# Four modulation pieces of state-space groups 0 to 2 computed beside the value products, in buffers reserved for the softmax rows

## The chip, the cores and the metric

The kernel runs on one core of a Trainium2 chip. The metric is device time in microseconds (us) of one launch. Five engines work beside each other, each through its own queue of instructions in order: TensorE (PE; its weight loads are counted apart as PEld), VectorE (DVE), ScalarE (ACT), GpSimd (POOL) and SyncE (SP), which here issues most DMAs. An instruction that waits holds back all that stands behind it on its engine.

## The reference, cut to what matters

One layer over 512 latent tokens and 256 context tokens, width 1024:

```
mod = silu(c) @ w_mod + b_mod                 # 6 x 1024 modulation values
sh1, sc1, gt1, sh2, sc2, gt2 = split(mod, 6)
h_lat, h_ctx = modulate(x, norm1_g, sh1, sc1), modulate(ctx, ...)
p = h @ w_in                                  # z | x,B,C | dt | q | k | v | gates
ssd  = ssd_bidir(...)                         # 4 groups of 8 heads, chunks of 128 tokens
att  = window_ctx_attention(q, k, v, ...)     # 16 heads, 4 for k and v
x = x + gt1 * ((g_ssd*(ssd @ w_o_ssd) + g_att*(att @ w_o_att)) @ w_out)
x = x + gt2 * conv_ffn(modulate(x, norm2_g, sh2, sc2))
return rmsnorm(x, final_g)
```

The first two of the six parts of `mod` (sh1, sc1) are needed at the start; the other four (gt1 on) only after both branches are merged. `w_mod` for these four is 16 MB.

## The kernel before

**Products.** Matrices are in fp32. Every product is made from two rounded halves of each operand: high × high, high × low, low × high (L197, L198, L200). A 512 KB piece of weights is loaded by SP into a ring of three buffers (`wraw`, L145); ScalarE casts it to the high half `whi` (L149), VectorE subtracts to get the low half `wlo` (L150). In attention the same pair of operations stands at L941 and L944. `hlh`, `hll`, `hch`, `hcl` are the halves of the normalised latent and context tokens, already transposed.

**Stages.** Start and modulation of the first part to 54 us; first products for q and k to 77 us; value products 77 to 95.8 us; attention to about 330 us with other products between; the output of attention; the four state-space groups g0 to g3, about 405 to 735 us; merging, output, the feed-forward part. "q2" and "q3" below are the third and fourth weight piece of q, loaded by SP ahead of attention.

**The modulation pieces.** The late four parts of `mod` are 32 pieces of 512 KB, and `m_step(i)` (L571) does one. VectorE multiplies the rows by silu(c) and adds into one tile `tm`: L581 for the first half of the first piece, L583 for each later half, so two operations a piece. After every fourth piece TensorE transposes `tm` in four blocks into a PSUM bank (L591), VectorE reduces that bank to `mod` (L593) and adds the bias (L594). In g0, g1 and g2 three pieces each are done (0 to 8), through the ring `wraw`; the rest follows after the groups.

**Value products** (`v_step`): six row blocks of the tokens, each accumulated in a PSUM bank of its own, five of the pool `mis` and one of the pool `acc` (L693 to L695). Afterwards ScalarE rounds each bank to the high half (L699) and copies 64 further columns (`te`, L701), and VectorE forms the low half (`vst`, L700).

**PSUM.** Eight banks. Up to the value products: three of `acc`, five of `mis`. At the start of attention the pools are laid out anew: two of `acc`, one tile of two banks for the scores, three for transposed probabilities, one for the outputs. The two banks of the scores are the third `acc` bank and the first `mis` bank of the old layout.

**Attention** follows an order written by a planner: scores (L811), softmax rows `p` (L820, L827; seven buffers of 640 columns), transposition to `pth` (L847, L851), product with the values (L860).

**A state-space group** is a list of steps (`prog`). `chunk_in` makes decays: ScalarE adds the time sums (L1465, L1468), VectorE selects (L1469), ScalarE takes the exponential (L1470), VectorE multiplies with the inner products of C and B (L1471), in two halves of four heads. `chunk_out` multiplies with the states (L1480), then with the eight heads' inputs (L1486), and advances the state (L1385, on POOL L1387, and L1388). `chunk_sum` transposes a part onto it (L1504) and multiplies with z (L1506). In between stand the projections of the next group with their convolution (L1267 to L1276) and the modulation pieces. L1365 squares the gated output for the norm. Outside attention the order of the engines' instructions is made by the framework from the order of the program, with a few anchors.

Of the kernel before, what the change touches and what calls it, by code (L numbers as in the profile page):

```python
# [9 lines left out]
F32 = mybir.dt.float32  # L10
F32R = mybir.dt.float32r
U8 = mybir.dt.uint8
AF = mybir.ActivationFunctionType
ALU = mybir.AluOpType
# [4 lines left out]
P = 128  # L19
D = 1024  # L20
L = 512
# [18 lines left out]
def raw(ap):  # L40
    return ap.bitcast(F32)
# [3 lines left out]
def tile_hybrid_layer(  # L45
# [32 lines left out]
    nc = tc.nc  # L78
    V, S, G, T = nc.vector, nc.scalar, nc.gpsimd, nc.tensor
# [17 lines left out]
    def bank(name):  # L97
        pool, w, tag = banks_[name]
        return pool.tile([P, 512 * w], F32, tag=tag, name=tag)
# [8 lines left out]
    def accb():  # L108
        return bank("acc")

    def misb():
        return bank("mis")
# [3 lines left out]
    def tmp(tag):  # L116
        return tpool.tile([P, 512], F32, tag=tag, name=tag, bufs=TMP[tag])
# [21 lines left out]
        src["up", i] = wup[i], 1024  # L139
    src["dn", 0] = wdn[0, 0], 1024  # L140

    def load_raw(key):
        a, n = src[key]
        r = wpool.tile([P, 1024], F32, tag="raw", name="wraw", bufs=3)
        nc.sync.dma_start(r[:, :n], a)  # L145
        return r, n

    def split(r, n, hi, lo):
        S.copy(hi[:, :n], r[:, :n])  # L149
        V.tensor_tensor(lo[:, :n], r[:, :n], raw(hi[:, :n]), ALU.subtract)  # L150

    def split_first(r, n, hi, lo):
        V.tensor_copy(hi[:, :n], r[:, :n])
# [150 lines left out]
    with tc.tile_pool(name="spool", bufs=1) as sp:  # L304
# [131 lines left out]
        r, W, H = {}, {}, {}  # L436
# [50 lines left out]
        rows = {}  # L487
# [47 lines left out]
        for i in range(NG):  # L535
            t = tmp("tb")
# [33 lines left out]
    def m_step(i):  # L570
        cg, kk = i // 4, i % 4  # L571

        def fn(r):
            if kk == 0:
                macc[0] = tmp("tm")
            acc = macc[0]
            for u in range(2):
                k = 2 * kk + u
                sc = csil[:, k, 0:1]
                if k == 0:  # L580
                    V.tensor_scalar_mul(acc, r[:, 0:512], sc)  # L581
                else:
                    V.scalar_tensor_tensor(acc, r[:, u * 512 : u * 512 + 512], sc, acc, ALU.mult, ALU.add)  # L583
            if kk == 3 and cg > 5:
                ps = misb()
                T.matmul(ps, ones, acc, start=True, stop=True)
                V.tensor_tensor(F["g2"][cg - 6], ps, F["g2"][cg - 6], ALU.add)
            elif kk == 3:
                ps = misb()
                for c in range(4):  # L590
                    T.transpose(ps[:, c * P : (c + 1) * P], acc[:, c * P : (c + 1) * P], ident)  # L591
                z = slice(4 * cg, 4 * cg + 4)
                V.tensor_reduce(mod2[:, z], ps.rearrange("p (c q) -> p c q", c=4), axis=AX.X, op=ALU.add)  # L593
                V.tensor_tensor(mod2[:, z], mod2[:, z], vec[:, V_BMOD + 16 + 4 * cg : V_BMOD + 20 + 4 * cg], ALU.add)  # L594

        return [("m", i)], fn
# [5 lines left out]
    a2p = a2pool.enter_context(tc.tile_pool(name="a2pool", bufs=1, reuse_waits="tile"))  # L602
# [59 lines left out]

        return [("k", t)], fn

    Q, F = {}, {}

    def q_high(r, t):
        q = [attp.tile([P, L], F32R, tag="q", name="q", bufs=7) for _ in range(2)]
# [3 lines left out]
    def q_low(r, t):  # L672

        q = Q[2 * t], Q[2 * t + 1]
        lo = tmp("tc").bitcast(F32R)
        V.tensor_tensor(lo, r, raw(q[0]), ALU.subtract)
        for o, i in ((q[1][64:128, :], q[0][64:128, :]), (q[1][0:64, :], lo[64:128, :]), (q[0][64:128, :], lo[0:64, :])):
            nc.sync.dma_start(raw(o), raw(i))

    def q_split(ps, t):  # L680
        r = rope(ps, 1.0)
        q_high(r, t)
        q_low(r, t)

    def v_step(*w):

        pos = [misb() for _ in range(5)] + [accb()]
        for k in range(KT):
            wh, wl = (z[:, (k % 3) * 320 : (k % 3 + 1) * 320] for z in w[k // 3])
            for t, po in enumerate(pos):  # L690
                hh, hl, c0 = (hlh, hll, t) if t < 4 else (hch, hcl, t - 4)
                c, o = slice(c0 * P, (c0 + 1) * P), po[:, 0:320]
                T.matmul(o, hh[:, k, c], wh, start=k == 0, stop=False)  # L693
                T.matmul(o, hh[:, k, c], wl, start=False, stop=False)
                T.matmul(o, hl[:, k, c], wh, start=False, stop=k == KT - 1)  # L695
        steps = tmp("te")
        for t, po in enumerate(pos):
            o = po[:, 0:256].rearrange("p (h d) -> p h d", h=4)
            S.copy(vst[:, t, :, 0:64], o)  # L699
            V.tensor_tensor(vst[:, t, :, 64:128], o, raw(vst[:, t, :, 0:64]), ALU.subtract)  # L700
            S.copy(steps[:, t * 64 : (t + 1) * 64], po[:, 256:320])  # L701
        F["steps"] = steps
# [86 lines left out]
    def block_atoms(n, turned):  # L789
# [27 lines left out]
        def least(i):  # L817
            h = 4 * j + i
            p = d["p"][i] = a2p.tile([P, 640], F32, tag="p", name="p", bufs=NP_)
            V.tensor_tensor_reduce(  # L820
# [57 lines left out]
        def of(k, back):  # L878

            return divmod(k - back, 4) if k >= back else None  # L880

        for i in range(4):
# [5 lines left out]
            needs = ["S%d.%d" % (n, i)] + (["c%d" % (n - 2)] if n > 1 else [])  # L888
            if k >= NP_:
                f, g = of(k, NP_)  # L890
                needs.append("T%d.%d.%d" % (f, (3, 4, 4, 3)[f % 4], g))
# [323 lines left out]

        return some

    NP_ = 7
    BESIDE = [("q", 2), ("q", 3), ("z", 0), ("z", 1), ("k", 1), ("q", 4), ("z", 2), ("z", 3), ("q", 5), ("z", 4)]
    BESIDE += [("q", 6), ("z", 5), ("z", 6), ("q", 7)] + [("z", i) for i in range(7, 14)] + [("oa", 0), ("oa", 1)]  # L1220
    OLD = len(BESIDE)
# [68 lines left out]
    def turn(n=None):  # L1290

        for t, n_, put in TURN[:n]:
            ps = misb()
            for c in range(n_):
                T.transpose(ps[:, c * P : (c + 1) * P], t[:, c * P : (c + 1) * P], ident)
            put(ps)
        del TURN[:n]

    def proj_steps(g):
        d = GR[g]  # L1300

        def b_fn(w):
            d["xs"] = bp.tile([P, 4, 512], F32, tag="xs", name="xs", bufs=2)
            d["xsc"] = bp.tile([P, 2, 512], F32, tag="xsc", name="xsc", bufs=1)
            d["Bkc"] = bp.tile([P, 2, P], F32, tag="Bkc", name="Bkc", bufs=2)
            d["Bk"] = bp.tile([P, 4, P], F32, tag="Bk", name="Bk", bufs=2)
            d["BT"] = bp.tile([P, L], F32, tag="BT", name="BT", bufs=2)
            pl, pc = accb(), accb()
            gemm([LAT(pl)], w)
            turn()  # L1310
            gemm([CTX(pc)], w)
            conv_silu(pl, L, 16 + g, d["BT"])
            BTc = tmp("tc")
            conv_silu(pc, LC, 16 + g, BTc)
            for t, n, k in ((d["BT"], 4, d["Bk"]), (BTc, 2, d["Bkc"])):
                TURN.append((t, n, lambda ps, n=n, k=k: S.copy(flat(k), ps[:, : n * P])))

        def c_fn(w):
            d["CT"] = bp.tile([P, L], F32, tag="CT", name="CT", bufs=2)
            pl = accb()  # L1320
            gemm([LAT(pl)], w)
            turn()
            conv_silu(pl, L, 20 + g, d["CT"])

        def x_fn(ct, w):
            i = 4 * g + ct
            pl, pc = accb(), accb()
            gemm([LAT(pl)], w)
            turn()
            gemm([CTX(pc)], w)  # L1330
            for pp, n, dst in ((pl, L, d["xs"]), (pc, LC, d["xsc"])):
                xl = tmp("tc")
                conv_silu(pp, n, i, xl)
                TURN.append(
                    (
                        xl,
                        n // P,
                        lambda ps, n=n, dst=dst: S.copy(
                            dst[:, :, ct * P : (ct + 1) * P], ps[:, :n].rearrange("p (a b) -> p a b", b=P)
                        ),  # L1340
                    )
                )

        r = [([("x", 16 + g)], b_fn), ([("x", 20 + g)], c_fn)]
        for ct in range(4):
            r.append(([("x", 4 * g + ct)], lambda w, ct=ct: x_fn(ct, w)))
        return r
# [173 lines left out]
        return r + [([], gate)]  # L1521

    msteps = [m_step(i) for i in range(32)]
    prog = proj_steps(0)
    for g in range(4):
        s = ssd_steps(g)
        f = fill[n2 + g : n2 + 1 + g]
        b = proj_steps(g + 1) if g < 3 else fill[n2 + 4 : n3]
        m = msteps[3 * g : 3 * g + 3] if g < 3 else []

        prog += s[0:1] + f + b[0:1] + s[1:2] + m[0:1] + b[1:2]
        for c in range(4):
            prog += s[3 * c + 2 : 3 * c + 3] + (s[3 * c + 4 : 3 * c + 5] if c < 3 else [])
            if g == 3 and c:
                prog += s[3 * c : 3 * c + 1]
            prog += b[2 + c : 3 + c]
            if c == 1:
                prog += b[6:]
            if g < 3 or c == 3:
                prog += s[3 * c + 3 : 3 * c + 4]  # L1540
            if c in (1, 2):
                prog += m[c : c + 1]
        prog += s[13:14]
# [649 lines left out]
```

## Time and profile before

| | us |
|---|---|
| median of 3 runs | 1231.55 |
| lowest, highest | 1231.36, 1231.83 |
| the profiled execution, its whole time | 1231.67 |
| the profiled execution, its span | 1229.8 |
| mean granted clock of TensorE | 0.998 |
| busy: TensorE, its weight loads | 1217.2, 996.6 |
| busy: VectorE, ScalarE, POOL | 914.8, 687.1, 168.0 |

The span runs from the first to the last instruction; the whole time has 1.87 us more around it. "Busy" sums the time of an engine's instructions. In rows of the timeline, the first number is the start and the second the time to the end of the last of so many (x) instructions; the bracket gives the idle time before and what released the instruction. Since instructions are pipelined, a row's end can lie a little behind the next row's start.

### The profile page before, as it was taken

Reading aid. Unit: us, or ns where it says so; the run is one execution under the profiler, and the core shown is the slowest. Engines: PE = TensorE matmul, PEld = TensorE weight load, DVE = VectorE, ACT = ScalarE, POOL = GpSimd, SP = SyncE. Lnnn points to the kernel's source line nnn. Section 1 sums busy time; section 2 is a strip of 40 time slices with the busy share of each in tenths; the row PEclk is TensorE's granted clock in tenths of the full one; section 3 lists DMA queues with packets and bytes.
Section 4 is the critical chain, followed back from the end, with each engine's and each line's share of the span. In section 5 each row is a group of like instructions: output and inputs, shape, how many; then the busy total and the mean of one; then the engine's idle time right before and its main releaser. Section 6 shows DMA issues by size and latency. Waiting matters only on the chain.

```text
span 1229.8 us, 17483 instructions
## 1 busy us (share of the span) xinstructions
PE 1217.2 (99%) x6337; PEld 996.6 (81%) x6337; DVE 914.8 (74%) x1489; ACT 687.1 (56%) x1302; POOL 168.0 (14%) x174
## 2 busy tenths in 40 slices
PE   9999999999999999999999999999999999999997
PEld 6798888888878877777777778888988888888886
DVE  4757888888654698697886786677688788886557
ACT  4657788787443556566586572223544444545543
POOL 0000111121100033233352530000200000000000
PEclk9999999999999999999999999999999999999999
DMA  9653678777846235345346466677144444457785
GB/s 359 250 149 91 216 203 190 213 193 218 219 143 208 92 126 147 117 131 184 122 140 201 137 204 221 230 242 236 50 164 147 145 151 152 153 169 244 245 303 200
DMA packets 108630, 224.65 MB, mean 183 GB/s; under 512 B 9600, under 2 KB 48832, under 8 KB 108544
## 3 DMA queue, kind: packets, MB, share of 16 engines
q1 hardware_dynamic: 101056, 197.32, 49.0%
q0 software_dynamic: 6912, 25.17, 8.7%
q8 instruction: 50, 0.82, 0.3%
q10 hardware_dynamic: 576, 1.05, 0.2%
q14 instruction: 36, 0.29, 0.1%
HBM read 193.29 MB, written 49.87 MB: 198 GB/s over the span
## 4 chain that ended last, share of the span: by engine, by line
PE 92%; DVE 3%; DMA 2%; ACT 2%; issue 1%; SPq 0%; POOLq 0%; ACTq 0%; DVEq 0%
PE acc L197 19%; PE acc L200 19%; PE acc L198 19%; PE acc L1919 3%; PE acc L1917 3%; PE acc L1918 3%; PE score L811 3%; PE po L860 3%; PE pt L847 2%; PE mis L1480 2%; PE mis L1385 2%; DMA wm<-wm 1%; PE acc L930 1%; PE mis L422 1%; PE acc L931 1%; PE acc L932 1%
## 5 line engine op out<-in xcount | busy, mean ns | idle before, releaser
L197 PE MATMUL acc<-hlh,whi 128*128 128x512 f32 x488 | 199.3, 408 | 0.0
L150 DVE TENSOR_TENSOR wlo<-wraw,whi 128x1024 fp32r<-128x1024 f32 (+2 forms) x119 | 143.4, 1207 | 70.1 <-ACT whi L149 60.8
L200 PE MATMUL acc<-hlh,wlo 128*128 128x512 f32 x488 | 191.4, 392 | 0.0
L149 ACT CAST whi<-wraw 128x1024 fp32r<-128x1024 f32 (+2 forms) x119 | 122.6, 1033 | 122.4 <-PE acc L198 74.5
L198 PE MATMUL acc<-hll,whi 128*128 128x512 f32 x488 | 190.8, 391 | 0.0
L197 PE MATMUL acc<-mh,whi 128*128 128x512 f32 x360 | 141.0, 392 | 0.0
L200 PE MATMUL acc<-mh,wlo 128*128 128x512 f32 x360 | 140.1, 389 | 0.0
L198 PE MATMUL acc<-ml,whi 128*128 128x512 f32 x360 | 140.0, 389 | 0.0
L200 PEld LDWEIGHTS acc<-hlh,wlo 128*128 128x128 f32 x488 | 91.6, 188 | 20.4
L198 PEld LDWEIGHTS acc<-hll,whi 128*128 128x128 f32 x488 | 91.9, 188 | 17.5 <-issue 1.7
L197 PEld LDWEIGHTS acc<-hlh,whi 128*128 128x128 f32 x488 | 91.8, 188 | 17.6 <-issue 2.2
L198 PEld LDWEIGHTS acc<-ml,whi 128*128 128x128 f32 x360 | 67.6, 188 | 14.5 <-issue 0.5
L197 PEld LDWEIGHTS acc<-mh,whi 128*128 128x128 f32 x360 | 67.6, 188 | 14.4 <-issue 0.5
L200 PEld LDWEIGHTS acc<-mh,wlo 128*128 128x128 f32 x360 | 67.6, 188 | 14.0
L820 DVE CUSTOM_DVE_ANT_0 p<-score,winm,nsink 128x512 f32<-128x512 f32 (+1 forms) x64 | 51.8, 810 | 15.0 <-PE score L811 13.6
L1268 DVE SCALAR_TENSOR_TENSOR ta<-acc,half,ta 128x511 f32<-128x511 f32 (+1 forms) x66 | 43.8, 663 | 25.8 <-ACT ta L1267 25.8
L1267 ACT ACTIVATE ta<-acc,half 128x512 f32<-128x512 f32 (+1 forms) x66 | 46.8, 709 | 27.1 <-PE acc L200 25.9
L1275 ACT ACTIVATE tb<-ta 128x512 f32<-128x512 f32 (+1 forms) x44 | 23.5, 534 | 65.0 <-DVE ta L1269 59.0
L827 ACT ACTIVATE p<-p,mneg 128x512 f32<-128x512 f32 (+1 forms) x64 | 49.7, 777 | 15.3 <-DVE mneg L820 14.7
L1387 POOL TENSOR_TENSOR st<-st,eT 128x512 f32<-128x512 f32 x24 | 33.5, 1396 | 170.6 <-ACT st L1405 162.3
L197 PE MATMUL acc<-hch,whi 128*128 128x256 f32 x176 | 54.4, 309 | 0.0
L855 DVE TENSOR_TENSOR ptl<-pt,pth 128x512 fp32r<-128x512 f32 x72 | 47.5, 686 | 8.6 <-ACT pth L851 7.8
(512 smaller groups left out, 2972.7 us busy)
## 6 DMA issues: line engine op xcount, KB each, us to landing
wraw<-wup SPq DMA_DIRECT2D x44, 512.0 KB, 3.6
wt_d<-wdn POOLq DMA_DIRECT2D x36, 512.0 KB, 7.5
fb<-cs_d SPq DMA_DIRECT2D x32, 512.0 KB, 6.6
wraw<-wm SPq DMA_DIRECT2D x32, 512.0 KB, 4.3
wraw<-wx SPq DMA_DIRECT2D x24, 512.0 KB, 3.5
wraw<-wt_d SPq DMA_DIRECT2D x20, 512.0 KB, 4.3
sp_d<-te SPq DMA_DIRECT2D x33, 256.0 KB, 2.5
wm<-wm SPq DMA_DIRECT2D x16, 512.0 KB, 7.7
```

The costliest lines, as they stand in the source:

```text
L149: S.copy(hi[:, :n], r[:, :n])
L150: V.tensor_tensor(lo[:, :n], r[:, :n], raw(hi[:, :n]), ALU.subtract)
L197: T.matmul(ps, wh, xh[:, k0 + k, :], start=a, stop=False)
L198: T.matmul(ps, wh, xl[:, k0 + k, :], start=False, stop=False)
L200: T.matmul(ps, wl, xh[:, k0 + k, :], start=False, stop=b)
L811: T.matmul(ps[:, o : o + len(z) * P], Q[h][:, b * P : (b + 1) * P], k[:, j, z[0] * P : (z[-1] + 1) * P], start=v == 0 and o % 512 in (0, P ...
L820: V.tensor_tensor_reduce(p[:, :w], d["ps"][i][:, o0 : o0 + w], m, op0=ALU.add, op1=ALU.min, scale=1.0, scalar=nsink[:, h : h + 1], accum_o ...
L827: S.activation(p, p, AF.Exp, bias=d["mneg"][:, i : i + 1], scale=-1.0, accum_out=d["den"][:, i : i + 1])
L855: V.tensor_tensor(d["ptl"][x], d["pt"][x], raw(d["pth"][x]), ALU.subtract)
L860: T.matmul(d["po"], vst[:, cols[x], j, :], d[y][x], start=x == 0 and y == "pth", stop=x == c - 1 and y == "ptl")
L1267: S.activation(o[:, :n], ps[:, :n], AF.Identity, scale=hcol(base_w, stride + i), bias=hcol(base_b, i))
L1268: V.scalar_tensor_tensor(o[:, 1:n], ps[:, 0 : n - 1], hcol(base_w, i), o[:, 1:n], ALU.mult, ALU.add)
```

## The change

Pieces 0 to 3 are done in `v_step`. Their eight half rows (128 x 512 floats, 256 KB each) are loaded by SP into six `p` buffers and two `pth` buffers, which are otherwise first used by the softmax; the value products are then issued (`v_products`), then the four pieces with an anchor that places VectorE's operations behind the low half of the last v weights, then the rounding of the values (`v_rows`). The groups get the remaining pieces: g0 4 to 6, g1 piece 7, g2 piece 8. So g1's places for its second and third piece, and g2's, are empty; the four transposes that stood in g2 now stand in g1 ahead of its first chunk, where those of pieces 0 to 3 had been.

```diff
+    F = {}
     def split(r, n, hi, lo):
         S.copy(hi[:, :n], r[:, :n])
-        V.tensor_tensor(lo[:, :n], r[:, :n], raw(hi[:, :n]), ALU.subtract)
+        F["low"] = V.tensor_tensor(lo[:, :n], r[:, :n], raw(hi[:, :n]), ALU.subtract)
...
             acc = macc[0]
+            rows = r if isinstance(r, list) else [r[:, u * 512 : u * 512 + 512] for u in range(2)]
...
                 if k == 0:
-                    V.tensor_scalar_mul(acc, r[:, 0:512], sc)
+                    V.tensor_scalar_mul(acc, rows[0], sc)
                 else:
-                    V.scalar_tensor_tensor(acc, r[:, u * 512 : u * 512 + 512], sc, acc, ALU.mult, ALU.add)
+                    V.scalar_tensor_tensor(acc, rows[u], sc, acc, ALU.mult, ALU.add)
...
+    NP_ = 7
+
     def v_step(*w):
 
-        pos = [misb() for _ in range(5)] + [accb()]
+        pieces = []
+        for i in range(4):
+            if i < 3:
+                r = [a2p.tile([P, 640], F32, tag="p", name="p", bufs=NP_)[:, :L] for _ in range(2)]
+            else:
+                r = [raw(a2p.tile([P, L], F32R, tag="pth", name="pth", bufs=2)) for _ in range(2)]
+            for u in range(2):
+                nc.sync.dma_start(r[u], wm2[0, i, :, u * L : u * L + L])
+            pieces.append(r)
+        behind = F["low"].ins
+        v_products(w)
+        with tc.issue_after(behind):
+            for i in range(4):
+                m_step(i)[1](pieces[i])
+        v_rows()
+
+    def v_products(w):
+
+        pos = F["pos"] = [misb() for _ in range(5)] + [accb()]
...
+
+    def v_rows():
         steps = tmp("te")
-        for t, po in enumerate(pos):
+        for t, po in enumerate(F.pop("pos")):
...
     msteps = [m_step(i) for i in range(32)]
+    mfirst = {0: msteps[4:7], 1: msteps[7:8], 2: msteps[8:9], 3: []}
...
-        m = msteps[3 * g : 3 * g + 3] if g < 3 else []
+        m = mfirst[g]
```

The lines of the changed kernel lie 2 to 25 further down: L591, L593 and L594 become L594, L596 and L597; L581 and L583 become L584 and L586; L693 to L695 become L716 to L718; L700 becomes L725; L811 becomes L836.

The first place is the end of the value products on TensorE, into the first score. Brackets name what an instruction waits for (DMA queues, or an engine). Before:

```order
L695 MATMUL mis<-whi,hcl 128x320
L693 MATMUL acc<-whi,hch 128x320
L694 MATMUL acc<-wlo,hch 128x320
L695 MATMUL acc<-whi,hcl 128x320
L811 MATMUL score<-khi,q 128x256 [waits DMAHW7_49,DMAHW4_49,Activation_49]
L811 MATMUL score<-klo,q 128x256 [waits DMAHW6_49]
```

Now:

```order
L718 MATMUL mis<-whi,hcl 128x320
L716 MATMUL acc<-whi,hch 128x320
L717 MATMUL acc<-wlo,hch 128x320
L718 MATMUL acc<-whi,hcl 128x320
L594 MATMUL mis<-ident,tm 128x128 [waits Activation_49]
L594 MATMUL mis<-ident,tm 128x128 x3
L836 MATMUL score<-khi,q 128x256 [waits DMAHW5_49,DMAHW1_49,DVE_49]
L836 MATMUL score<-klo,q 128x256 [waits DMAHW3_49]
```

The four transposes stand between the last value product and the first score, and the score's wait is for VectorE where it was for ScalarE.

VectorE over the same stretch. Before:

```order
L150 TENSOR_TENSOR wlo<-wraw,whi 128x640
L944 TENSOR_TENSOR wlo<-wraw,whi 128x1024
L700 TENSOR_TENSOR vst<-mis,vst 128x4x64 x5
L700 TENSOR_TENSOR vst<-acc,vst 128x4x64
L820 ISA p,mneg<-score,winm,nsink 128x512
```

Now:

```order
L152 TENSOR_TENSOR wlo<-wraw,whi 128x640
L584 TENSOR_SCALAR tm<-p,csil 128x512
L586 SCALAR_TENSOR_TENSOR tm<-p,csil,tm 128x512 x5
L586 SCALAR_TENSOR_TENSOR tm<-pth,csil,tm 128x512 x2
L969 TENSOR_TENSOR wlo<-wraw,whi 128x1024
L725 TENSOR_TENSOR vst<-mis,vst 128x4x64 x5
L725 TENSOR_TENSOR vst<-acc,vst 128x4x64
L596 TENSOR_REDUCE mod_89<-mis 128x4
L597 TENSOR_TENSOR mod_89<-mod_89,vec 128x4
L845 ISA p,mneg<-score,winm,nsink 128x512
```

Eight accumulation steps come ahead of the next weights' low half, and the reduction with its add comes behind the six low halves of the values.

The second place is VectorE at the second chunk (chunk 1) of g1. Before:

```order
L1373 TENSOR_TENSOR xw<-xs,TD 128x512
L583 SCALAR_TENSOR_TENSOR tm<-wraw,csil,tm 128x512 x2
L1469 COPY_PREDICATED E<-sel,eb 128x512
L1471 TENSOR_TENSOR E<-E,mis 128x512
L1469 COPY_PREDICATED E<-sel,eb 128x512
L1268 SCALAR_TENSOR_TENSOR ta<-acc,half,ta 128x511
L1471 TENSOR_TENSOR E<-E,mis 128x512
L1269 SCALAR_TENSOR_TENSOR ta<-acc,half,ta 128x511
L1268 SCALAR_TENSOR_TENSOR ta<-acc,half,ta 128x255
L1506 TENSOR_TENSOR z<-mis,z 128x4x128
```

Now:

```order
L1397 TENSOR_TENSOR xw<-xs,TD 128x512
L1493 COPY_PREDICATED E<-sel,eb 128x512
L1495 TENSOR_TENSOR E<-E,mis 128x512
L1493 COPY_PREDICATED E<-sel,eb 128x512
L1292 SCALAR_TENSOR_TENSOR ta<-acc,half,ta 128x511
L1495 TENSOR_TENSOR E<-E,mis 128x512
L1293 SCALAR_TENSOR_TENSOR ta<-acc,half,ta 128x511
L1530 TENSOR_TENSOR z<-mis,z 128x4x128
L1292 SCALAR_TENSOR_TENSOR ta<-acc,half,ta 128x255
```

The two accumulation steps ahead of the first selection are gone, and the product with z stands ahead of the 255 columns of the convolution. In g2's chunk 1 the product with z moves ahead of the same operation.

The third place is SP behind the last value weights. Before:

```order
L145 DMA wraw<-wv 128x640
L678 DMA q<-q 64x512
L145 DMA wraw<-wq 128x1024
L678 DMA q<-tc 64x512 x2
L646 DMA khi<-khi 64x768 x2
```

Now, from the loads of the pieces on:

```order
L699 DMA p<-wm 128x512 x4
L147 DMA wraw<-wv 128x640
L699 DMA p<-wm 128x512
L681 DMA q<-q 64x512
L699 DMA p<-wm 128x512
...
L681 DMA q<-tc 64x512 x2
L699 DMA pth<-wm 128x512 x2
L147 DMA wraw<-wq 128x1024 x2
L147 DMA wraw<-wz 128x1024 x2
```

The load of q2 (the first of the two `wq` rows) came right behind the value weights, and comes behind the copies of k and q and the two `pth` loads now.

More of the change, by code (lines that the diff above doesn't have):

```diff
@@ L663, in k_step @@
         return [("k", t)], fn
-    Q, F = {}, {}
+    Q = {}
     def q_high(r, t):
@@ L1216, in weight_sums @@
         return some
-    NP_ = 7
     BESIDE = [("q", 2), ("q", 3), ("z", 0), ("z", 1), ("k", 1), ("q", 4), ("z", 2), ("z", 3), ("q", 5), ("z", 4)]
```

## The prediction

> **What bounds the kernel now.** I read the page first: the span, and the chain that ended last by engine.
>
> ```profile
> span 1229.8 us, 17483 instructions
> PE 92%; DVE 3%; DMA 2%; ACT 2%; issue 1%; SPq 0%; POOLq 0%; ACTq 0%; DVEq 0%
> ```
>
> TensorE holds 92% of the chain, so an edit changes the time only where TensorE waits, or by work on TensorE itself. The rest is read from the timelines of each engine at the places where the order differs: the end of the value products, and two places in groups 1 and 2 (g0 to g3 below) of the state-space part. The timeline's columns are start, duration, engine, line and operation, and in brackets the idle time before it with what ended it. The handover from the value products to attention on TensorE, VectorE and ScalarE:
>
> ```profile
> 95.68 0.31 PE L695 MATMUL acc<-whi,hcl 128*128 128x320 f32 x1
> 95.83 0.28 PE L811 MATMUL score<-khi,q 128*128 128x256 f32 x1
> ...
> 83.58 0.83 DVE L150 TENSOR_TENSOR wlo<-wraw,whi 128x640 fp32r<-128x640 f32 x1 [2.05 <-ACT whi L149]
> 91.87 1.23 DVE L944 TENSOR_TENSOR wlo<-wraw,whi 128x1024 fp32r<-128x1024 f32 x1 [7.46 <-ACT whi L941]
> 94.23 2.18 DVE L700 TENSOR_TENSOR vst<-mis,vst 128x256 fp32r<-128x256 f32 x5 [1.13 <-ACT vst L699]
> 96.77 0.74 DVE L820 CUSTOM_DVE_ANT_0 p<-score,winm,nsink 128x512 f32<-128x512 f32 x1
> ...
> 90.79 1.05 ACT L941 CAST whi<-wraw 128x1024 fp32r<-128x1024 f32 x1 [7.24 <-PE acc L695]
> 93.82 0.81 ACT L699 CAST vst<-mis 128x256 fp32r<-128x256 f32 x2 [1.98 <-PE mis L695]
> 94.69 0.21 ACT L701 COPY te<-mis 128x64 f32<-128x64 f32 x1
> ```
>
> TensorE passes from value product to score without a gap (95.68 to 95.83). The bank of the first score was last read at 94.69 + 0.21 = 94.90, by ScalarE. VectorE has 7.46 us of idle time ahead of L944.
>
> **The change part by part.** *Eight accumulation steps enter the 7.46 us gap.* The same steps later in the program give their durations; the last row is the table by stretch (length; busy us of TensorE, its weight loads, VectorE, ScalarE, POOL; granted clock, DMA share, GB/s):
>
> ```profile
> 813.97 0.48 DVE L581 TENSOR_SCALAR tm<-wraw,csil 128x512 f32<-128x512 f32 x1
> 814.48 2.33 DVE L583 SCALAR_TENSOR_TENSOR tm<-wraw,csil,tm 128x512 f32<-128x512 f32 x3
> ...
> 533.41 2.33 DVE L583 SCALAR_TENSOR_TENSOR tm<-wraw,csil,tm 128x512 f32<-128x512 f32 x2
> 532.83 1.59 POOL L1387 TENSOR_TENSOR st<-st,eT 128x512 f32<-128x512 f32 x1
> ...
> 84.40:91.80 7.40, 7.40 (x53) 7.40 (x52) 0.01 (x1) 1.01 (x1) 0.00 (x0) 1.00 0.49 163
> ```
>
> The first step takes 814.48 − 813.97 = 0.51, each dependent one 2.33 / 3 = 0.78; eight make 0.51 + 7 × 0.78 = 6.0, from 83.58 + 0.83 = 84.41 to 90.4. L944 waits until ScalarE is done at 90.79 + 1.05 = 91.84 anyway, so the price is nothing: that idle time hides it, and POOL does nothing there. Without that cover, at the 2.33 / 2 = 1.17 a step that the pair beside a POOL operation took, the eight end at 84.41 + 0.51 + 7 × 1.17 = 93.1. L944 would end 93.1 + 1.23 = 94.3, about when the value lows begin (94.23), so even then no more than 0.1 is lost. Below nothing it cannot go, as nothing is removed here.
>
> By the Trainium skill ("SBUF — State Buffer", section "Who interferes with whom") a VectorE instruction with two SBUF inputs contends with a GpSimd instruction that reads SBUF, and the later one waits. By this rule the pair in g1 waited for POOL until 532.83 + 1.59 = 534.42 and then took its two steps to 535.98; the trace has 535.74, so it agrees within 0.3, and no step near 84 us would wait. The sum by the rule is 6.0, by the slower pair 8.7, and the price 0 or 0.1.
>
> *Four transposes and a reduction enter the handover.* The transposes write the bank that the first score takes. In the new order the first score therefore waits for VectorE's reduction, where it waited for ScalarE's copy, and that reduction stands behind all six value lows on VectorE. Prices come from the same operations later in the program:
>
> ```profile
> 631.71 0.60 PE L591 MATMUL mis<-ident,tm 128*128 128x128 f32 x4
> 632.15 1.88 PE L1480 MATMUL mis<-st,CT 128*128 128x512 f32 x4
> L593 DVE TENSOR_REDUCE mod<-mis 128x4 f32<-128x512 f32 x6 | 4.1, 678 | 0.0
> ```
>
> The transposes take 632.15 − 631.71 = 0.44 and run at 95.83 to 96.27, before VectorE is free. VectorE takes the next operation after the lows at 96.77 (now L820); the reduction goes there and ends at 97.45. TensorE follows about 0.05 later (in g1 a product starts at 540.78 after a VectorE end at 540.73, rows below), so the first score starts at 97.50 instead of 95.83: **+1.67**. Queued behind it on TensorE is all of attention, and there the engine is busy throughout:
>
> ```profile
> 96.00:330.00 234.00, 233.95 (x1286) 199.91 (x1286) 189.00 (x392) 184.41 (x360) 36.88 (x64) 1.00 0.71 190
> ```
>
> It is busy 233.95 of 234.00 us, so no later wait shrinks when the score comes late, and nothing gives the 1.67 back. The four transposes vanish from g2, where TensorE was busy with them: **−0.44**. The reduction's own add behind it delays only VectorE's next operation, which has to wait for the score in any case. Bounds of this part: −0.44 (no wait at all) to 1.67 − 0.44 + 0.74 = +1.97 (VectorE takes its next operation, 0.74, ahead of the reduction).
>
> *Loads.* Eight DMAs of 256 KB (128 x 512 floats) go out on SP. Four are queued ahead of the last value weights, four behind, and q2's weights leave after the last two:
>
> ```profile
> 69.43 0.33 SPq L145 DMA_DIRECT2D wraw<-wv  x1
> 72.86 0.34 SPq L145 DMA_DIRECT2D wraw<-wq  x1
> 84.31 0.58 SPq L145 DMA_DIRECT2D wraw<-wq  x1
> wraw<-wq SPq DMA_DIRECT2D x2, 512.0 KB, 4.1
> ```
>
> The last value weights went out at 69.43 and their low half is formed at 83.58; four issues of 0.33 and a landing of about 4 leave some 8 us. Before, q2 went out at 72.86 and q3 at 84.31. Now q2 leaves after two issues of about 0.34 at 84.31, so at 85.0 to 85.6, and lands 4.1 later, 89.1 to 89.7. L941 takes it at 90.79 now, and would delay the value copies only if it began after 93.82 − 1.05 = 92.77. Price 0, the cover is 3 us; the DMA engines were busy 0.49 of that stretch. Beyond the cover each us late is a us lost (rival C).
>
> *Group 1, chunk 1 loses the pair of accumulation steps.*
>
> ```profile
> 534.34 0.40 ACT L1468 ACTIVATE eb<-fb,TX 128x128 f32<-128x128 f32 x1
> 535.66 0.74 DVE L1469 COPY_PREDICATED E<-sel,eb 128x512 f32<-128x512 uint8 x1
> 540.04 0.69 DVE L1471 TENSOR_TENSOR E<-E,mis 128x512 f32<-128x512 f32 x1
> 541.44 0.48 DVE L1268 SCALAR_TENSOR_TENSOR ta<-acc,half,ta 128x255 f32<-128x255 f32 x1
> 541.84 0.68 DVE L1506 TENSOR_TENSOR z<-mis,z 128x512 f32<-128x512 f32 x1
> 539.23 0.66 PE L1486 MATMUL mis<-E,xs 128*64 128x128 f32 x8
> 540.78 0.66 PE L1486 MATMUL mis<-E,xs 128*64 128x128 f32 x8 [0.90 <-DVE E L1471]
> 541.37 1.13 PE L1385 MATMUL mis<-xw,Bk 128*128 128x512 f32 x2
> 542.58 0.49 PE L1449 MATMUL mis<-CT,BT 128*128 128x128 f32 x2
> ...
> 636.56 0.49 PE L1449 MATMUL mis<-CT,BT 128*128 128x128 f32 x2
> 635.57 1.12 PE L1385 MATMUL mis<-xw,Bk 128*128 128x512 f32 x2 [0.52 <-DVE z L1506]
> ```
>
> L1469 waits for ScalarE's 534.34 + 0.40 = 534.74, and stood behind the pair until 535.66. Freed, it starts at 534.79, 0.87 earlier. The chain from it (exponential, second half, multiplication at 540.04) moves with it, since ScalarE's own queue follows L1469. TensorE's second eight products would follow the first at 539.23 + 0.59 = 539.82, and started at 540.78: a wait of 0.96, of which **−0.87**. What is late next is ScalarE. Further, z (L1506) now stands ahead of the 255-wide L1268, 0.40 earlier; L1449 waited for the bank that z reads (541.84 + 0.68 = 542.52). L1385 to L1449 took 1.21 here and 0.99 in g2 (635.57 to 636.56): **−0.22**.
>
> *Group 2, chunk 1 loses transposes, reduction and steps.*
>
> ```profile
> 620.07 1.09 PE L1486 MATMUL mis<-E,xs 128*64 128x128 f32 x16
> 621.09 1.12 PE L1385 MATMUL mis<-xw,Bk 128*128 128x512 f32 x2
> 633.96 1.09 PE L1486 MATMUL mis<-E,xs 128*64 128x128 f32 x16
> ...
> 634.45 0.47 DVE L1268 SCALAR_TENSOR_TENSOR ta<-acc,half,ta 128x255 f32<-128x255 f32 x1
> 634.84 0.67 DVE L1506 TENSOR_TENSOR z<-mis,z 128x512 f32<-128x512 f32 x1
> ```
>
> The sixteen products took 621.09 − 620.07 = 1.02 one chunk earlier, and 635.57 − 633.96 = 1.61 here, with L1385 waiting for z: 0.59 too much. z moves ahead of the 0.39 of L1268, and the reduction and a ScalarE square ahead of it go as well: **−0.59**. Bounds for both groups together: 0 (other waits take their place) to −1.77 (all of 0.96, 0.22 and 0.59 go); I take the sum of the three, since each wait's next releaser is named and earlier.
>
> The sum is 1.67 − 0.44 − 0.87 − 0.22 − 0.59 = −0.45 against the profiled execution, whose run took 1231.67, 1.87 around a span of 1229.8. The median of the runs is 1231.55, so the forecast is 1231.55 − 0.45 = **1231.1 us**. g0 keeps three pieces, other ones, and its waits.
>
> **The rivals.** *A: the score waits, and the groups give nothing back.* ScalarE or the next VectorE operation replaces each wait; in g1's third chunk two ScalarE copies come ahead of an exponential. For it: each group place is a chain through two engines. Against it: ScalarE has the idle time, and z's move is in the order itself. Time 1231.55 + 1.67 − 0.44 = 1232.8.
>
> *B: the score does not wait.* VectorE gets to the reduction early because the value lows are done sooner, or the score's bank is another than I read. For it: the lows idle 1.13 us on ScalarE. Against it: that idle time is ScalarE's and not VectorE's, and the order names VectorE as the score's releaser. Time 1231.55 − 0.44 − 0.87 − 0.22 − 0.59 = 1229.4.
>
> *C, the slower side: q2's weights are late.* SP issues it behind two piece loads and the copies of the rotated rows. If the two loads of the last piece, q2, q3 and z0 (4 × 512 KB = 2.1 million bytes) share 163 GB/s from 84.3, the last byte lands at 84.3 + 12.9 = 97.2. L941 then ends at about 98.2, and the value copies behind it on ScalarE come 98.2 − 93.82 = 4.4 late; time 1231.1 + 4.4 = 1235.5. It decides from a landing after 92.77. For it: the value products' own weights and the copies are in flight too. Against it: 4.1 us for 512 KB in the row above, with the same queue behind it.
>
> **How the numbers follow.** Chances: forecast 0.67, A 0.17, B 0.07, C 0.09. The forecast's own bounds are 1231.1 + 0.7 and, if the groups' waits go wholly (−1.77 for −1.68), 1231.0; A and B are its bounds with a whole part gone. So the range is 1229.6 to 1232.9: the forecast, A and the upper part of B, somewhat over 8 in 10, with C and the outer part of B left out. Two tenths of a per cent (2.46 us) is what this measurement can tell from no change. Only the lower part of B with a little of the forecast's tail lies below 1229.1 (0.05), C and a little of A lie above 1234.0 (0.10), the rest counts as the same (0.85).
>
> **What would show it.** Right: on TensorE about 1.2 us of idle time between the four transposes and the first score, ended by VectorE's reduction of mod; eight accumulation steps between 84.4 and 90.5, none above 0.8, and the low half at L944 (L969 of the changed kernel) still released by ScalarE; in g1 the second eight L1486 products with a wait under 0.1; in g2 L1385 without a wait on z. Wrong: a first score within 0.2 of the transposes (B); the 0.90 and 0.52 waits still there under other names (A); ScalarE's cast of q2 after 92.8 (C). It would also be wrong if attention caught the 1.67 up, or if groups 0 and 3, where pieces are other ones or none, changed in length.

## The result, and the profile after

| | before | changed |
|---|---|---|
| median (lowest, highest), 7 runs each | 1231.73 (1231.36, 1232.55) | 1235.89 (1234.29, 1236.36) |
| span of the profiled execution | 1229.8 | 1232.7 |

The ratio is 1.0028, with a 95% interval of 1.0019 to 1.0038: slower, where 0.45 us faster was forecast and 1232.9 was the upper end of the range. One run of 1514.4 in the bank experiment below and one of 3149.1 with half the wait were in a slow state, and are left out of all numbers. The runs of the changed kernel lie in two clusters, three at 1234.3 to 1234.5 and four at 1235.9 to 1236.4; the profiled execution (1234.5) is one of the lower cluster. So there are two questions: where its 2.9 us come from, and what the upper cluster adds.

The page of the changed kernel, its span and the chain that ended last by engine:

```profile
span 1232.7 us, 17504 instructions
PE 88%; DVE 6%; ACT 2%; DMA 2%; issue 1%; POOL 0%; SPq 0%; POOLq 0%; ACTq 0%; DVEq 0%
```

VectorE has doubled its share of the chain, from 3% to 6%. The timeline at the handover from the values to attention:

```profile
95.47 0.31 PE L718 MATMUL acc<-whi,hcl 128*128 128x320 f32 x1
95.61 0.60 PE L594 MATMUL mis<-ident,tm 128*128 128x128 f32 x4
97.29 0.39 PE L836 MATMUL score<-khi,q 128*128 128x256 f32 x1 [1.08 <-DVE mod L596]
...
84.63 3.90 DVE L586 SCALAR_TENSOR_TENSOR tm<-p,csil,tm 128x512 f32<-128x512 f32 x5
88.57 1.54 DVE L586 SCALAR_TENSOR_TENSOR tm<-pth,csil,tm 128x512 f32<-128x512 f32 x2
91.78 1.22 DVE L969 TENSOR_TENSOR wlo<-wraw,whi 128x1024 fp32r<-128x1024 f32 x1 [1.68 <-ACT whi L966]
96.56 0.68 DVE L596 TENSOR_REDUCE mod<-mis 128x4 f32<-128x512 f32 x1
...
90.70 1.05 ACT L966 CAST whi<-wraw 128x1024 fp32r<-128x1024 f32 x1 [7.36 <-DMA wraw<-wq]
```

This is the place as it was drawn: eight steps done at 90.1, the low half still released by ScalarE, and the score behind the reduction. From the last value product to the score it is 97.29 − 95.47 = 1.82, where it was 0.15: +1.67. New is that ScalarE's cast of q2 was released by its DMA in this execution, at 90.70, some 2 us ahead of harm.

The first product of the down part of the feed-forward, in the kernel before and then in the changed one (TensorE, and VectorE and ScalarE in the changed one):

```profile
1112.98 0.39 PE L200 MATMUL mis<-mh,wlo 128*128 128x512 f32 x1
1113.21 0.39 PE L1917 MATMUL acc<-ww,fyh 128*128 128x512 f32 x1
```

```profile
1113.02 0.39 PE L202 MATMUL mis<-mh,wlo 128*128 128x512 f32 x1
1115.94 0.47 PE L1942 MATMUL acc<-ww,fyh 128*128 128x512 f32 x1 [2.53 <-DVE tc L1836]
...
1113.45 0.78 ACT L1834 ACTIVATE tc<-mis,vec 128x512 f32<-128x512 f32 x1 [1.18 <-PE mis L202]
1115.05 0.75 DVE L1836 SCALAR_TENSOR_TENSOR tc<-mis,vec,tc 128x511 f32<-128x511 f32 x1
```

Here, some 440 us behind the end of g2, the last stretch that the change touches, TensorE idles 2.5 us. The products are the same and in the same order; the difference is a wait. In the list of instructions with their waits, before and now:

```
L200 MATMUL mis<-mh,wlo 128x512
L1917 MATMUL acc<-ww,fyh 128x512

L202 MATMUL mis<-mh,wlo 128x512
L1942 MATMUL acc<-ww,fyh 128x512 [waits DVE_49,Activation_49]
```

The values waited for are those of the two readers of the last up product (L1834 on ScalarE and L1836 on VectorE, which end at 1114.23 and 1115.80). The kernel changes its PSUM layout at this point, from five banks `mis` and three `acc` to eight `acc` (`psum_pools(acc=(8, 1))`), and the first down product takes bank 0. In the built program before, the last up product lies in bank 1; in the changed one in bank 0 (the bank experiment below tests this). The pool gives each new tile one of its free banks, and since the transposes of a modulation piece have left group 2, the `mis` tiles behind them come to lie in other banks.

Where the 2.9 us went, stretch by stretch, from the starts of TensorE's instructions in both profiled executions. A group is counted from a projection's first products to the next group's (428.67, 508.71, 590.02 and 670.30 before; 429.95, 510.00, 591.11 and 670.22 now):

| stretch of TensorE | before | changed | difference | forecast |
|---|---|---|---|---|
| start to last value product | 95.68 | 95.47 | −0.21 | 0 |
| last value product to first score | 0.15 | 1.82 | +1.67 | +1.67 |
| first score to g0 | 332.84 | 332.66 | −0.18 | 0 |
| g0 | 80.04 | 80.05 | 0.01 | 0 |
| g1 | 81.31 | 81.11 | −0.20 | −1.09 |
| g2 | 80.28 | 79.11 | −1.17 | −1.03 |
| g3 to last up product | 442.68 | 442.80 | +0.12 | 0 |
| last up to first down product | 0.23 | 2.92 | +2.69 | 0 |
| first down product to the end | 116.59 | 116.76 | +0.17 | 0 |

In g1 the two waits of chunk 1 went, as forecast; so did the one in g2. TensorE of the changed kernel at both places:

```profile
540.52 1.09 PE L1510 MATMUL mis<-E,xs 128*64 128x128 f32 x16
541.54 1.12 PE L1409 MATMUL mis<-xw,Bk 128*128 128x512 f32 x2
542.50 0.38 PE L1473 MATMUL mis<-CT,BT 128*128 128x128 f32 x2
...
634.61 1.09 PE L1510 MATMUL mis<-E,xs 128*64 128x128 f32 x16
635.64 1.12 PE L1409 MATMUL mis<-xw,Bk 128*128 128x512 f32 x2
```

But two new waits came in the last chunk of g1. VectorE, POOL and TensorE of the changed kernel there:

```profile
559.36 1.48 DVE L584 TENSOR_SCALAR tm<-wraw,csil 128x512 f32<-128x512 f32 x1 [0.41 <-DMA wraw<-wm]
560.76 1.26 DVE L1480 SCALAR_TENSOR_TENSOR coef<-TT,cbd,bcs 128x8 f32<-128x8 f32 x1
561.94 1.84 DVE L586 SCALAR_TENSOR_TENSOR tm<-wraw,csil,tm 128x512 f32<-128x512 f32 x1
563.70 0.74 DVE L1493 COPY_PREDICATED E<-sel,eb 128x512 f32<-128x512 uint8 x1
...
559.25 1.31 POOL L1390 TENSOR_TENSOR ssq<-ssq,sq 128x512 f32<-128x512 f32 x1
560.50 1.49 POOL L1519 TENSOR_TENSOR dx<-dx,te 128x512 f32<-128x512 f32 x1
561.96 1.27 POOL L1390 TENSOR_TENSOR ssq<-ssq,sq 128x512 f32<-128x512 f32 x1
...
567.09 1.12 PE L1504 MATMUL mis<-st,CT 128*128 128x512 f32 x2 [0.45 <-ACT xs L1362]
569.41 0.66 PE L1510 MATMUL mis<-E,xs 128*64 128x128 f32 x8 [0.61 <-DVE E L1495]
```

Three VectorE operations took 1.48, 1.26 and 1.84 us beside POOL's chain; where POOL did nothing, the same three took 0.47, 0.22 and 0.75 (at 525.34, 520.73 and 525.86 in the kernel before). In the kernel before, the squares were summed on POOL earlier (553.13 to 556.09), ahead of this place, and only one of the two steps stood ahead of the first selection:

```profile
561.34 1.27 DVE L583 SCALAR_TENSOR_TENSOR tm<-wraw,csil,tm 128x512 f32<-128x512 f32 x1 [0.63 <-DMA wraw<-wm]
562.53 0.73 DVE L1469 COPY_PREDICATED E<-sel,eb 128x512 f32<-128x512 uint8 x1
563.15 0.74 DVE L583 SCALAR_TENSOR_TENSOR tm<-wraw,csil,tm 128x512 f32<-128x512 f32 x1
```

### The profile page after: what moved, and what is told of

It reads as the page before. It is cut to its first block, busy times and chain, and to the rows that moved or that the text cites. A ratio compares the mean times of both kernels' runs of the same rounds, so it can differ in the third digit from the quotient of the medians.

```text
span 1232.7 us, 17504 instructions
## 1 busy us (share of the span) xinstructions
PE 1217.9 (99%) x6337; PEld 996.9 (81%) x6337; DVE 915.9 (74%) x1489; ACT 687.0 (56%) x1302; POOL 167.7 (14%) x174
## 4 chain that ended last, share of the span: by engine, by line
PE 88%; DVE 6%; ACT 2%; DMA 2%; issue 1%; POOL 0%; SPq 0%; POOLq 0%; ACTq 0%; DVEq 0%
PE acc L199 18%; PE acc L202 18%; PE acc L200 18%; PE acc L1942 3%; PE acc L1944 3%; PE acc L1943 3%; PE score L836 3%; PE po L885 3%; PE pt L872 2%; DMA wm<-wm 1%; PE mis L1504 1%; PE acc L955 1%; PE mis L1409 1%; PE acc L956 1%; PE acc L957 1%; PE mis L424 1%
```

## The experiments

**The bank.** The layout ahead of the down products is changed so that the first accumulator lies on bank 1 and bank 0 is used a whole product later. The same two edits went into the changed kernel and into the kernel before, where the last up product is on bank 1.

```diff
-        psum_pools(acc=(8, 1))
+        psum_pools(low=(1, 1), acc=(7, 1))
...
-            m, f_ = [accb(), accb()], [accb()]
+            m, f_ = [accb(), accb()], [bank("low")]
```

In the changed kernel:

> The changed kernel, with the eight PSUM banks of the down products laid out so that the first accumulator sits on bank 1 and no longer on bank 0 (one edit in the layout and one in the list of accumulators; the arithmetic is the same). Theory: the 2.5 us in which TensorE idles ahead of the first down product (1113.25 to 1115.94 in the changed kernel) is the wait for the bank in which the last up product was accumulated, bank 0 now, until VectorE has read it. It vanishes here, and the profiled span falls from 1232.7 by 2.5 to 2.7, to about 1230.1. Rival: the wait is for the down weights' rounding on ScalarE or for code of TensorE, then it stays, and the span stays at 1232.7 or above.

Measured: span 1229.5, ratio 0.9999 (0.9990 to 1.0008), runs at 1231.3 to 1232.8. TensorE at the place:

```profile
1112.49 0.39 PE L202 MATMUL mis<-mh,wlo 128*128 128x512 f32 x1
1112.71 0.39 PE L1942 MATMUL acc<-ww,fyh 128*128 128x512 f32 x1
```

The wait is gone, and the changed kernel is level with the one before. The span is 3.2 below that of the changed kernel, where 2.5 to 2.7 was expected: 2.70 of it lie here, and the rest mainly ahead of the last value product (0.24) and in g0 (0.23), which these edits don't touch. So much can differ between two executions. In the kernel before:

> The kernel before, with exactly the same two edits. There the last up product was accumulated in bank 1, so that the edit puts the first down product onto it. Theory of the bank: TensorE idles 2.5 us there, in a kernel that has nothing else of the change; span 1229.8 + 2.6 = 1232.4, median about 1234.3. Rival (weights or code): no idle time, span 1229.8, median 1231.7.

Measured: ratio 1.0025 (1.0014 to 1.0035), runs at 1233.8 to 1234.4 and 1235.6 to 1236.3, the profiled span 1234.2, an execution of the upper cluster. TensorE at the place:

```profile
1112.95 0.39 PE L200 MATMUL mis<-mh,wlo 128*128 128x512 f32 x1
1115.87 0.47 PE L1917 MATMUL acc<-ww,fyh 128*128 128x512 f32 x1 [2.53 <-DVE tc L1811]
```

The same 2.53 us appear in a kernel that has nothing of the change but the shared bank. The edits that cure the one kernel harm the other, so neither the weights nor the layout with seven banks is the cause; the cause is which bank the two products share.

**The clusters.** I took the upper cluster for a late load of q2 first. The edit moves that load ahead:

```diff
     def v_step(*w):
+        RAW.append(load_raw(("q", 2)))
         pieces = []
...
-    RAW.append(load_raw(BESIDE[0]))
```

> The changed kernel, with the load of q2's weights issued ahead of the modulation pieces in the program, so that it goes out before the last p load and both pth loads. Question: runs of the changed kernel lie in two clusters, 1234.3 to 1234.5 and 1235.9 to 1236.4. Theory: in the upper cluster q2's load lands late (in the profiled execution of the lower one ScalarE's cast of it was already released by the DMA, at 90.7, with 1.9 us of cover left), and here all runs lie at 1234.3 to 1234.5, and the cast is released by something else. Rival: the clusters have another cause and stay, 1234.3 to 1236.4.

Measured: ratio 1.0026 (1.0016 to 1.0035), runs at 1234.2 to 1234.6 and 1235.4 to 1237.6. ScalarE's cast was released by TensorE again, as before the change, and the clusters stayed. The theory of q2 falls:

```profile
90.90 1.05 ACT L968 CAST whi<-wraw 128x1024 fp32r<-128x1024 f32 x1 [7.24 <-PE acc L720]
```

The edit is not needed for that releaser: TensorE also released the cast in the profiles of the bank experiment (at 90.34) and of the upper cluster below (at 90.54), which both load q2 as the changed kernel does. What the edit did move is a `pth` load: the last accumulation step waited 1.80 for it and began at 91.92, and the first score still came 1.82 behind the last value product.

The profile of the kernel before on the shared bank had pointed to another cause: eight products at nearly twice their spacing behind the wait. So the wait was halved, and the changed kernel was run again beside that.

```diff
-        psum_pools(acc=(8, 1))
+        psum_pools(low=(1, 1), acc=(7, 1))
...
-            m, f_ = [accb(), accb()], [accb()]
+            m, f_ = [accb(), bank("low")], [accb()]
```

> The changed kernel, with the down products' two accumulators laid out so that only the second of them sits on the bank of the last up product: six products (6 x 0.227 = 1.36 us) can run before the wait. Theory: the wait shrinks by that much, from 2.73 us of lost time to 1.37, so that the span is 1232.7 - 1.36 = 1231.3 (run time about 1233.1). And if it is the long idle time that brings the granted clock of TensorE down in some executions (eight products at 0.43 instead of 0.23 us behind the wait, in the profile of the earlier run with the two edits on the kernel before), a gap of half the length brings no second cluster: all runs lie within 1 us. Rival: the lower clock comes with any gap there, then a cluster about 1.7 us above stays, at 1234.8.

> The changed kernel itself once more, beside the run above. Theory: its runs lie in two clusters again, 1234.3 to 1234.6 and 1235.4 to 1236.5, and if the profiled execution is one of the upper cluster (span 1234.1 or more), its products behind the wait at 1113 to 1116 take 0.43 us for some 3.4 us, and nothing else differs from the first profile (span 1232.7) by more than 0.3 us. Rival: in the upper cluster the time is lost in another place.

Measured for half the wait: span 1231.1, median 1232.91, ratio 1.0010 (1.0001 to 1.0019), all runs of the comparison at 1232.7 to 1234.0. TensorE there:

```profile
1114.19 0.39 PE L1944 MATMUL acc<-ww,fyh 128*128 128x512 f32 x1
1115.76 0.47 PE L1942 MATMUL low<-ww,fyh 128*128 128x512 f32 x1 [1.18 <-DVE tc L1836]
```

The wait ends at the same moment relative to VectorE's reading, with six products ahead of it. The ten runs lie within 1.25 and not within 1, since two of them (1233.8 and 1234.0) lie above the other eight (1232.7 to 1233.2). But there is no cluster 1.7 higher, and all ten show a mean granted clock of 0.998 or 0.999.

Measured for the changed kernel again: ratio 1.0026 (1.0015 to 1.0038), runs at 1234.4 to 1234.5 and 1235.6 to 1236.2. This time the profiled execution was one of the upper cluster, span 1234.1. TensorE behind the wait:

```profile
1115.78 0.76 PE L1942 MATMUL acc<-ww,fyh 128*128 128x512 f32 x1 [2.53 <-DVE tc L1836]
1116.34 0.63 PE L1943 MATMUL acc<-ww,fyl 128*128 128x512 f32 x1
1116.77 0.63 PE L1944 MATMUL acc<-ww,fyh 128*128 128x512 f32 x1
...
1118.90 0.49 PE L1943 MATMUL acc<-ww,fyl 128*128 128x512 f32 x1
1119.23 0.39 PE L1944 MATMUL acc<-ww,fyh 128*128 128x512 f32 x1
```

and the table by stretch, with the granted clock in the third column from the right:

```profile
1116.00:1118.90 2.90, 2.90 (x7) 2.23 (x8) 2.90 (x5) 1.55 (x3) 0.00 (x0) 0.50 0.62 237
```

The clock is 0.50 for some three microseconds. From 1115.78 to 1119.23 eight products passed in 3.45 us, for 8 × 0.227 = 1.82 at full clock: 1.6 us lost. The wait ended 0.16 earlier than in the first profile (1115.94), and the first product was slow there too, by 0.1; that leaves 1.4, the difference of the spans (1234.1 to 1232.7). In the first profile of the changed kernel the granted clock of the stretch just behind the wait is 1.00:

```profile
1116.70:1120.20 3.50, 3.50 (x17) 2.87 (x16) 3.50 (x8) 2.15 (x5) 0.00 (x0) 1.00 0.71 220
```

So the idle time can cost a second time, through the clock. Of the 31 executions with the whole wait (the changed kernel twice, the kernel before on the shared bank, and the run with q2's load ahead), 18 took 1235.4 us or more. Four of these 31 were profiled: two of the upper cluster, both with the half clock behind the wait (0.50 from 1117.0 to 1120.2 in the kernel before on the shared bank), and two of the lower, both without.

The mean granted clock of the whole execution, which every run has, says more of the others. Some 3.2 us at half clock take 0.0013 off it. It is 0.998 in all 13 lower runs, and 0.996 or 0.997 in 15 of the 18 upper ones. Of the other three, two (1235.45 and 1235.61) show 0.998 and one (1237.57) 0.947: they lost time in a way that stays open. Without the wait, 0.997 is rare: none of the ten runs of the bank experiment on the changed kernel, and 2 of the 40 runs of the kernel before that stood beside these. That the half clock lies behind the wait in the 13 lowered executions that were not profiled is inferred.

The Trainium skill ("TensorE: Matmul & The Clock Gate", section "What's actually happening") says that the clock falls to a half after an idle window of about 3.4 us, that this window runs freely, and that it takes a busy window to come back. The half clock (0.50) and its length (3.2 to 3.5 us here) agree, and a window that runs freely would make it a matter of chance. The idle time that sufficed here was 2.5 us by the profile's bracket (2.9 from start to start), less than the page's window; the measurement decides.

**The score's wait.** With the bank of the down products mended, the four transposes are moved to a bank that the scores don't take: that of the second row block of the values, which belongs to the attention's outputs afterwards. `m_close` holds the transposes, the reduction and the add that stood in `m_step`.

```diff
-                m_step(i)[1](pieces[i])
+                m_step(i)[1](pieces[i], False)
+        bank7 = F["pos"][1]
         v_rows()
+        m_close(0, macc[0], bank7)
```

> The kernel of the bank experiment (changed kernel with the down products moved off the bank), and in addition the four transposes of the modulation at the end of the value products write the bank of the second row block of the values once it has been read, and no new one; that bank belongs to the attention's outputs and not to its scores. Theory: the first score no longer waits for VectorE's reduction. The 1.08 us of idle time between transposes and score goes, and the rest of the program keeps its lengths: span 1229.5 - 1.1 = 1228.4. Rival: the reduction still stands ahead of the first softmax row on VectorE (0.68 + 0.16), attention waits for it a few products later, and less than 0.4 us is gained: span 1229.1 or more.

Measured: span 1228.2, ratio 0.9990 (0.9981 to 0.9999). TensorE and VectorE at the handover:

```profile
95.46 0.60 PE L574 MATMUL mis<-ident,tm 128*128 128x128 f32 x4
95.81 0.36 PE L840 MATMUL score<-khi,q 128*128 128x256 f32 x1
...
96.41 0.68 DVE L576 TENSOR_REDUCE mod<-mis 128x4 f32<-128x512 f32 x1
97.20 0.74 DVE L849 CUSTOM_DVE_ANT_0 p<-score,winm,nsink 128x512 f32<-128x512 f32 x1
```

The score starts at 95.81, and the 1.3 us are kept to the end (1229.5 to 1228.2). The reduction still stands ahead of the first softmax row, which starts 0.4 later than before (97.20 to 96.77): nothing on TensorE waits for that.

**The last chunk of g1.** In addition to the two edits above, piece 8 goes from the start of g2, whose program overlaps the end of g1, to g2's second chunk.

```diff
-    mfirst = {0: msteps[4:7], 1: msteps[7:8], 2: msteps[8:9], 3: []}
+    mfirst = {0: msteps[4:7], 1: msteps[7:8], 2: [([], lambda: None), msteps[8]], 3: []}
```

> As the run beside it, and piece 8 of the modulation done in the second chunk of group 2 and not at its start, so that its two accumulation steps no longer lie beside the fourth chunk of group 1. Theory: in the changed kernel these two steps and the coefficient operation between them took 1.48, 1.26 and 1.84 us (0.48, 0.34 and 0.75 elsewhere) because POOL worked on the squares and on dx at the same time, and held back the selection behind them on VectorE; without them the waits of 0.6 and 0.9 us of TensorE in that chunk go: span 1.2 to 1.5 below the run beside it, about 1227.0. Rival: the waits come from ScalarE's order (two copies of xs ahead of the second exponential) and stay: span within 0.4 of the run beside it.

Measured: span 1227.1, ratio 0.9979 (0.9970 to 0.9988), median 1229.11 beside 1231.62: faster than the kernel before, by 2.5 us. g1 took 79.58 us, against 81.16 in the run beside it. The span fell by 1.1, a little less than expected: 0.45 of g1's gain is missing again in the stretch behind the first down product (117.05 for 116.6), which was not followed. VectorE, POOL and ScalarE at the place:

```profile
557.38 0.34 DVE L1484 SCALAR_TENSOR_TENSOR coef<-TT,cbd,bcs 128x8 f32<-128x8 f32 x1
559.49 1.31 DVE L1497 COPY_PREDICATED E<-sel,eb 128x512 f32<-128x512 uint8 x1 [1.78 <-ACT eb L1496]
...
558.90 1.31 POOL L1523 TENSOR_TENSOR dx<-dx,te 128x512 f32<-128x512 f32 x1
560.15 1.78 POOL L1394 TENSOR_TENSOR ssq<-ssq,sq 128x512 f32<-128x512 f32 x1
...
562.84 0.56 ACT L1366 COPY xs<-mis 128x512 f32<-128x512 f32 x1
564.25 0.62 ACT L1498 ACTIVATE E<-E 128x512 f32<-128x512 f32 x1
```

Both waits are gone. ScalarE's copies still come ahead of the second exponential, and POOL still sums the squares beside, so the rival (ScalarE's order) falls: what held TensorE were the two steps in VectorE's queue ahead of the selection. How much of the 4.3 us that they and the coefficients between them took (559.36 to 563.70) was their slowness beside POOL is argued and not shown, since the steps and their slowness went together; by the durations it is 3.1 (1.01, 1.04 and 1.09 more than where POOL did nothing). The 0.34 of the expectation is no quiet duration: in the kernel before (560.37) and here (557.38) that operation ends when one of POOL does. The selection itself took 1.31 here, and ended 0.59 behind POOL's operation (560.80 to 560.21). That is as the Trainium skill has it ("SBUF — State Buffer", section "Who interferes with whom"), by which the later of the two waits for the shared port.

## Why the prediction was wrong, point by point

- **The step that failed** is the sum itself, which ended with g2: nothing behind it was given a term. "Four transposes ... vanish from g2" was costed as 0.44 us of TensorE, but they also gave up a PSUM tile, and later `mis` tiles moved to other banks, the last up product's from bank 1 to bank 0. That put the first down product on the bank of the last up product: +2.69, and in about half of the executions 1.4 more by the clock. With that one term removed the changed kernel ran at a median of 1232.3 (0.9999 of the kernel before), inside the range given but not at the 1231.1 forecast: without that term the stretches add up to +0.21, where −0.45 was forecast, mainly because of g1 (below). The term could have been seen ahead: the wait on L1942 stands in the list of instructions with their waits, which the prediction used at the edited places only.
- **The handover** was right: +1.67 forecast, +1.67 measured. The bank experiment on it moved 1.3 of it, so rival B (no wait) falls and the releaser is shown.
- **Eight steps hidden in the 7.46 us**: right. They ended at 90.1, forecast 90.4, with 0.78 a step.
- **q2's load**: the cover was there but smaller than forecast in one execution, where it released ScalarE at 90.70 and 89.1 to 89.7 was forecast; in others TensorE was later. Rival C did not come about; with the load moved ahead the time stayed.
- **g2**: −1.17 for −1.03, right.
- **g1**: the second term that was off. Chunk 1 was right, both waits went (539.23 to 542.58 before, 540.52 to 542.50 now: −1.37 for −1.09). But the sum of the group was −0.20, since two waits of 0.45 and 0.61 (by the brackets) came in the last chunk. For g1 alone that is rival A's result, by another mechanism: the place in the program was named (ScalarE's copies ahead of an exponential), and these were not the cause; piece 8's two steps ahead of the selection were.
- **Attention has no slack to give the 1.67 back**: nearly right, 0.18 came back by g0 (a wait of 0.20 of TensorE at 355 us in the kernel before is not there in the changed one).

## What to carry to other kernels

A tile that is no longer taken from a pool can move the banks of the tiles behind it. After such an edit, compare the waits of the whole program and not the order of instructions near the edit, above all where the pools are laid out anew. A new buffer for a small result should be taken from what is needed last, here the attention's output bank and not the score's: that was worth 1.3 us. And an idle gap of TensorE may cost more than its length.

## What the runs showed of the hardware

2.5 us of idle time on TensorE, in a program that otherwise keeps it busy, brought the granted clock to 0.50 for about 3 us in some executions, 1.4 us each in the profile; by the mean granted clock it was 15 of 31. At 1.2 us of idle time (half the wait) none of ten runs showed a lowered mean clock, and behind the 1.1 us of the score's wait the profile of the changed kernel shows the clock at 1.00. Where the limit lies between was not tried.
